# Small TensorE work between expert products in fewer, larger groups, and experts alternating in the last down product

## The chip, the cores and the metric

The kernel runs on one core of one Trainium2 chip. The metric is the device time of one execution in microseconds (us). Three executions of the kernel before took 1856.57, 1856.98 and 1857.13 us, a median of 1856.98 us. A fourth execution was profiled; all rows below come from it.

## The reference

Two layers work on 512 latent tokens and 256 context tokens of width 1024, in float32. Each layer mixes tokens (a bidirectional mLSTM, a convolution and a Fourier mixer between one input and one output projection) and then runs a mixture of 16 experts in which each expert chooses its tokens. The change touches the experts alone:

```python
def expert_choice_ffn(xn, w_router, w_gate, w_up, w_down):
    cap = EC_CAPACITY_FACTOR * n // N_EXPERTS            # 64 of 512 latent, 32 of 256 context tokens
    aff = softmax(xn @ w_router)
    gate, idx = top_k(swapaxes(aff, 1, 2), cap)
    xs = xn[idx]
    hid = silu(xs @ w_gate) * (xs @ w_up)                # each weight 1024 x 1024 per expert
    ys = (hid @ w_down) * gate[..., None]
    return zeros_like(xn).at[idx].add(ys)
...
    h_ctx = h_ctx + cgt2 * expert_choice_ffn(...)        # layer one only
    x = x + gt2 * expert_choice_ffn(...)
return _rms(x, g_final)                                  # after layer two
```

The second layer has no use for its context tokens, so only latent tokens pass its experts. The expert weights are 3 x 16 x 4 MB a layer, 403 MB in the two layers together, of the 513 MB that the kernel reads.

## The kernel before

Experts go in eight pairs p. A pair has three wide products, `gate`, `up` and `down`, each through `wide`, which takes the 1024-deep contraction in four quarters q. A quarter uses two weight tiles of 1 MB, one an expert. The products stand in the order gate 0, up 0, and then for each p: gate p+1, down p, up p+1. In layer one a quarter is 16 float32 matmuls for latent tokens (L1433), a call of `fill(q)`, and 8 matmuls for context tokens (L1443); each occupies 32 of the array's 128 columns, so that four groups of columns hold different products. In layer two it is 8 latent matmuls on 64 columns each (the two experts side by side) and then `fill(q)`. The profile counts each float32 matmul as two instructions.

What `fill` does is the small work, held in lists and taken by `pop`: `turns` fetch the next pair's tokens and transpose them (L1382 in layer one, four transposes and four evictions an item; in layer two `onehot`, L1364, and `turn` as a matmul with a one-hot matrix, L1379); `trans` transposes the hidden activations for the down product (L1485, items of four); `scat` adds results back to the token stream (`sc_`, L1498 on TensorE and L1499 on VectorE). All use the whole array, and each item takes a PSUM bank from `bank67`, banks 6 and 7 in turn. In layer one the first six pairs' results instead go to memory by accumulating indirect DMAs (`down_out`, L1537), and `collect` reads them back (`late`, transposed at L1554 from gate 7 on).

```python
up(0, lambda q: pop(turns))
...
        gate(p + 1, lambda q: (pop(scat), q and pop(trans)))
...
        up(p + 1, lambda q: (q and pop(scat, 2), pop(turns)))
```

The last pair of layer two ends in `down_last`, which makes the down product by quarters qd of 256 output columns. A quarter is 16 matmuls at L1693, in blocks of four: expert 0 for k 0 to 3, expert 1 for k 0 to 3, expert 0 for k 4 to 7, expert 1 for k 4 to 7, with `pop(scat)` behind each block. Quarters 0 and 1 share one PSUM bank, 2 and 3 another. Each quarter is evicted by ScalarE (L1699, the high part) and VectorE (L1700, the rest); `last_sum` then scatters two blocks of 128 columns (L1498, L1499) and squares them (L1675), and `rows` sums the squares on TensorE (L1683) for the final RMS norm, which the last quarter's squares end. After them come L359, L376, the scaling at L1747 and the output.

TensorE's order is the order of the code; the other engines' instructions are ordered by a scheduler. Weights come in one stream on SyncE's queue (L1146, and L1143 for the last pair's down): `load_experts` runs behind each quarter and reloads the buffers as the quarter that used them ends. Layer one has 11 such buffers, so a tile is asked for when the tile eleven places before it has been used; layer two has 16.

Of the kernel before, what the change touches and what calls it, by code (L numbers as in the profile page):

```python
# [15 lines left out]
KB = 8  # L16
# [139 lines left out]
def build(nc, tc, xT, ctxT, params, w_ada, w_gates, w_in, w_out, w_router, w_e_gate, w_e_up, w_e_down,  # L156
# [6 lines left out]
    def body(A, RB, PS, scr, xrow, acc):  # L163
# [233 lines left out]
        for l in range(2):  # L397
# [735 lines left out]
            wtiles, wtaken = [], [0]  # L1133

            def load_experts(firsts=(), most=1000):
                while len(wtiles) < min(wtaken[0] + len(wreg), len(wq), most):
                    w, e, i = wq[len(wtiles)]
                    if last and w is w_e_down and e >= E - 2:
                        t = V(wreg[len(wtiles) % len(wreg)], KB, 256)
                        src = w[l, e, i].rearrange("p (k c) -> p k c", k=KB)  # L1140

                        for k0, k1 in ((0, KB),) if i < 3 else ((0, 4), (4, KB)):
                            sp.dma_start(t[:, k0:k1], src[:, k0:k1])  # L1143
                    else:
                        t = V(wreg[len(wtiles) % len(wreg)], 2, D)
                        r = sp.dma_start(t, w[l, e, i].rearrange("p (a f) -> p a f", a=2))  # L1146
                        after(r, firsts)
                    wtiles.append(t)
# [260 lines left out]

            def bank67():  # L1410
                six[0] += 1
                return B(6 + six[0] % 2)
# [249 lines left out]
            def down_last(p):  # L1662
# [23 lines left out]
                for qd in range(4):  # L1686
# [3 lines left out]
                    for k0 in (0, 4):  # L1690
                        for e in range(2):
                            for k in range(k0, k0 + 4):
                                pe.matmul(b[64 * e:64 * e + 64], hT[:, k, 64 * e:64 * e + 64], w[e][:, k],  # L1693
                                          start=k == 0, stop=k == KB - 1, tile_position=(0, 64 * e))
                            pop(scat)
                    pop(scat, 99)
                    c0 = qd * 256
                    h, lo = (YS[:, j, c0:c0 + 256] for j in range(2))
                    act.activation(h, b, AF.Copy, scale=GP[:, 0, p:p + 1])  # L1699
                    dve.scalar_tensor_tensor(lo, b, GP[:, 0, p:p + 1], h.bitcast(F32), op0=OP.mult, op1=OP.subtract)  # L1700
                    if qd == 2:
                        rows(range(4))
                    scat.extend(last_sum(db) for db in (2 * qd, 2 * qd + 1))
# [16 lines left out]
            up(0, lambda q: pop(turns))  # L1720
            for p in range(NP):
# [4 lines left out]
                if p + 1 < NP:  # L1726
                    fetch_pair(p + 2)
                    gate(p + 1, lambda q: (pop(scat), q and pop(trans)))
# [5 lines left out]
                if p + 1 < NP:  # L1734
                    up(p + 1, lambda q: (q and pop(scat, 2), pop(turns)))
# [109 lines left out]
```

## Time and profile before

| | |
|---|---|
| median of three executions | 1856.98 us |
| profiled execution | 1857.74 us |
| its span, first to last instruction | 1856.0 us |
| around the span | 1.74 us |
| TensorE busy, share of the span | 94% |
| experts of layer one, about | 482 to 1023 us |
| experts of layer two, about | 1368 to 1842 us |

A span counts from the first to the last instruction of the program. A matmul's end is modelled, so a TensorE that counts as busy may be slower than it could be.

### The profile page before, as it was taken

Reading aid. Unit: us, or ns where it says so; the run is one execution under the profiler, and the core shown is the slowest. Engines: PE = TensorE matmul, PEld = TensorE weight load, DVE = VectorE, ACT = ScalarE, POOL = GpSimd, SP = SyncE. Lnnn points to the kernel's source line nnn. Section 1 sums busy time; section 2 is a strip of 40 time slices with the busy share of each in tenths; the row PEclk is TensorE's granted clock in tenths of the full one; section 3 lists DMA queues with packets and bytes.
Section 4 is the critical chain, followed back from the end, with each engine's and each line's share of the span. In section 5 each row is a group of like instructions: output and inputs, shape, how many; then the busy total and the mean of one; then the engine's idle time right before and its main releaser. Section 6 shows DMA issues by size and latency. Waiting matters only on the chain.

```text
span 1856.0 us, 27692 instructions
## 1 busy us (share of the span) xinstructions
PE 1744.3 (94%) x11728; PEld 947.8 (51%) x11728; DVE 627.9 (34%) x1384; ACT 448.5 (24%) x862; POOL 166.0 (9%) x193
## 2 busy tenths in 40 slices
PE   7899999899899999999999989889989999999997
PEld 3678887676333333333233468777644444334433
DVE  4624897323201001001014567956230221121213
ACT  5423354313201101101000553346221001110001
POOL 1122120321101101101100001110000000000000
PEclk8999999899899999999999999999989999999998
DMA  9365344855899999999995112233659999999992
GB/s 346 115 208 193 106 133 137 314 188 209 350 419 402 411 412 403 399 421 391 393 393 217 35 54 79 76 108 129 250 240 421 420 420 421 420 421 420 421 420 99
DMA packets 100668, 529.59 MB, mean 285 GB/s; under 512 B 10176, under 2 KB 21440, under 8 KB 51648
## 3 DMA queue, kind: packets, MB, share of 16 engines
q1 hardware_dynamic: 81920, 459.66, 61.8%
q0 software_dynamic: 18624, 68.17, 11.7%
q8 instruction: 92, 1.51, 0.3%
q14 instruction: 32, 0.26, 0.0%
HBM read 513.10 MB, written 14.68 MB: 284 GB/s over the span
## 4 chain that ended last, share of the span: by engine, by line
PE 70%; DMA 10%; DVE 9%; issue 5%; ACT 2%; SPq 2%; POOL 1%; another core or an unknown queue 0%; DVEq 0%; POOLq 0%; ACTq 0%
PE PS L1433 29%; PE PS L490 16%; PE PS L1443 8%; PE PS L1379 3%; DVE A L1015 2%; PE PS L1498 2%; PE PS L284 1%; PE PS L1693 1%; SPq L309 1%; DMA accc<-A 1%; DMA WP<-w_e_up 1%; DMA A<-w_e_up 1%; DMA A<-w_e_down 1%; DMA A<-w_e_gate 1%; DMA WP<-w_e_gate 1%
## 5 line engine op out<-in xcount | busy, mean ns | idle before, releaser
L490 PE MATMUL PS<-RA,RB 128*128 128x512 f32 (+1 forms) x2352 | 516.4, 367 | 23.6 <-ACT A L973 8.0
L1433 PE MATMUL PS<-A 128*32 128x512 f32 (+1 forms) x2256 | 428.1, 594 | 2.7 <-DMA A<-w_e_up 2.2
L490 PEld LDWEIGHTS PS<-RA,RB 128*128 128x128 f32 x2352 | 379.3, 194 | 99.3 <-issue 20.6
L1433 PE MATMUL PS<-WP,A 128*32 128x512 f32 (+1 forms) x2160 | 373.9, 597 | 0.7 <-DMA WP<-w_e_up 0.7
L1433 PEld LDWEIGHTS PS<-A 128*32 128x32 f32 (+1 forms) x2256 | 128.0, 121 | 224.9 <-issue 213.7
L1433 PEld LDWEIGHTS PS<-WP,A 128*32 128x32 f32 (+1 forms) x2160 | 107.0, 117 | 192.7 <-issue 187.6
L1443 PE MATMUL PS<-WP,A 128*32 128x512 f32 x816 | 112.5, 595 | 0.0
L1015 DVE SCALAR_TENSOR_TENSOR A<-A 128x783 f32<-128x783 f32 (+1 forms) x120 | 107.4, 921 | 0.1
L1499 DVE SCALAR_TENSOR_TENSOR A<-PS,A 128x512 f32<-128x512 f32 x80 | 57.5, 748 | 130.5 <-PE PS L1498 130.5
L1387 ACT ACTIVATE A<-PS,A 128x128 f32<-128x128 f32 x80 | 36.4, 457 | 262.0 <-DVE A L1389 260.8
L1486 ACT ACTIVATE A<-PS 128x512 f32<-128x512 f32 x40 | 23.8, 597 | 306.2 <-PE PS L1485 306.0
L1389 DVE TENSOR_SCALAR A<-PS,A 128x128 f32<-128x128 f32 x80 | 32.6, 409 | 185.8 <-PE PS L1382 93.4
L1443 PE MATMUL PS<-A 128*32 128x512 f32 x656 | 95.3, 607 | 0.0
L422 ACT ACTIVATE RB<-A 128x1024 fp32r<-128x1024 f32 x60 | 63.2, 1057 | 128.4 <-PE PS L490 83.1
L1532 DVE TENSOR_SCALAR A<-PS,A 128x512 f32<-128x512 f32 x6 | 4.5, 750 | 245.6 <-PE PS L1433 245.6
L282 POOL DMA_DIRECT2D A<-w_ada x80 | 60.1, 754 | 211.2 <-PE PS L284 134.2
L1506 DVE SCALAR_TENSOR_TENSOR RB<-PS,A,RB 128x512 fp32r<-128x512 f32 x18 | 13.5, 750 | 163.7 <-ACT RB L1505 162.8
L1379 PE MATMUL PS<-A 128*128 128x128 f32 x512 | 64.0, 285 | 5.0 <-DVE A L1499 4.5
L425 DVE TENSOR_TENSOR RB<-A,RB 128x1024 fp32r<-128x1024 f32 x50 | 60.8, 1221 | 21.0 <-ACT RB L422 20.6
L1379 PEld LDWEIGHTS PS<-A 128*128 128x128 f32 x512 | 61.0, 199 | 12.9 <-DVE A L1499 9.8
L1443 PEld LDWEIGHTS PS<-WP,A 128*32 128x32 f32 x816 | 26.8, 109 | 50.8 <-issue 50.8
L1498 PE MATMUL PS<-RB 128*128 128x512 f32 x160 | 51.7, 431 | 1.0 <-DVE A L1499 0.4
(334 smaller groups left out, 1583.8 us busy)
## 6 DMA issues: line engine op xcount, KB each, us to landing
A<-w_e_gate SPq DMA_DIRECT2D x75, 1024.0 KB, 14.3
A<-w_e_up SPq DMA_DIRECT2D x66, 1024.0 KB, 13.0
WP<-w_e_down SPq DMA_DIRECT2D x63, 1024.0 KB, 14.3
A<-w_e_down SPq DMA_DIRECT2D x63, 1024.0 KB, 16.0
WP<-w_e_up SPq DMA_DIRECT2D x62, 1024.0 KB, 13.0
WP<-w_e_gate SPq DMA_DIRECT2D x53, 1024.0 KB, 14.9
A<-w_ada POOLq DMA_DIRECT2D x80, 512.0 KB, 5.5
A<-w_in SPq DMA_DIRECT2D x44, 512.0 KB, 3.7
```

The costliest lines, as they stand in the source:

```text
L282: after(eng.dma_start(w, src[r, hf, k]), firsts if hf == 0 and k < len(ring.regs) else ())
L422: whi.append(act.activation(h, raw[i], AF.Copy))
L425: wlo.append(eng.tensor_tensor(lo, raw[i], h.bitcast(F32), OP.subtract))
L490: pe.matmul(banks[s][:, :LEN[s]], w[:, k], xin[:, j, k, OFF[s]:OFF[s] + LEN[s]], start=k == k0 and i == 0, stop=k == k1 and i == 2)
L1015: dve.scalar_tensor_tensor(o, i, wcol, o, op0=OP.mult, op1=OP.add)
L1379: pe.matmul(b[:, j], XT[2 + c][:, db * 128:db * 128 + 128], onehots[i][:, c], start=c == 0, stop=c == 3)
L1387: act.activation(dst[:, db], b[:, j], AF.Identity, bias=sh_, scale=sc_)
L1389: dve.tensor_scalar(dst[:, db], b[:, j], sc_, sh_, op0=OP.mult, op1=OP.add)
L1433: pe.matmul(B(o + hf)[c:c + wd, :], lhs(k, e)[:, c % 64:c % 64 + wd], w[e][:, a, hf * 512:hf * 512 + 512], start=k == 0, stop=k == KB - 1, ...
L1443: pe.matmul(B(o + 2)[32 * g:32 * g + 32, :], lhsc(k, e), w[e][:, a, hf * 512:hf * 512 + 512], start=k == 0, stop=k == KB - 1, tile_positio ...
L1498: pe.matmul(b, YS[:, j, db * 128:db * 128 + 128], PM if pm is None else pm, start=j == 0, stop=j == 1)
L1499: dve.scalar_tensor_tensor(X[LAT][:, db], b, MOD[l][:, LAT, 40 + db:41 + db], X[LAT][:, db], op0=OP.mult, op1=OP.add)
```

## The change

It has four parts. First, the lists are popped at other quarters and more at a time. In layer one `turns` come two together behind quarters 0 and 2 of up, and of the three `trans` two come together behind quarter 1 of gate and one behind quarter 2. In layer two gate pops two `trans` at quarter 1, and up pops four `scat` and the one-hot item at quarter 1, and two `turns` and four `scat` at quarter 3. Second, `bank67` has four banks to go round in layer two. Third, `down_last` alternates the experts at every k, pops nothing inside a product, makes the first `rows` behind quarter 3 instead of 2, and pops each quarter's sums behind the next quarter's product. Fourth, the halves of the last two weight tiles are asked for in turn.

```diff
--- before.py
+++ after.py
@@ -1130,7 +1130,7 @@
             for q in range(NP):
                 order += [(w_e_gate, q + 1)] * (q + 1 < NP) + [(w_e_down, q)] + [(w_e_up, q + 1)] * (q + 1 < NP)
             wq = [(w, 2 * q + e, i) for w, q in order for i in range(4) for e in range(2)]
-            wtiles, wtaken = [], [0]
+            wtiles, wtaken, halves = [], [0], []
 
             def load_experts(firsts=(), most=1000):
                 while len(wtiles) < min(wtaken[0] + len(wreg), len(wq), most):
@@ -1139,8 +1139,14 @@
                         t = V(wreg[len(wtiles) % len(wreg)], KB, 256)
                         src = w[l, e, i].rearrange("p (k c) -> p k c", k=KB)
 
-                        for k0, k1 in ((0, KB),) if i < 3 else ((0, 4), (4, KB)):
-                            sp.dma_start(t[:, k0:k1], src[:, k0:k1])
+
+                        halves.append((t, src))
+                        if i < 3:
+                            sp.dma_start(*halves.pop())
+                        elif len(halves) == 2:
+                            for k0 in (0, 4):
+                                for t_, s_ in halves:
+                                    sp.dma_start(t_[:, k0:k0 + 4], s_[:, k0:k0 + 4])
                     else:
                         t = V(wreg[len(wtiles) % len(wreg)], 2, D)
                         r = sp.dma_start(t, w[l, e, i].rearrange("p (a f) -> p a f", a=2))
@@ -1407,9 +1413,12 @@
 
             six = [0]
 
+
+            small = (6, 2, 7, 5) if last else (6, 7)
+
             def bank67():
                 six[0] += 1
-                return B(6 + six[0] % 2)
+                return B(small[six[0] % len(small)])
 
             sets = [0]
 
@@ -1687,19 +1696,21 @@
                     w = wtiles[wtaken[0]:wtaken[0] + 2]
                     wtaken[0] += 2
                     b = B(o + qd // 2)[:, qd % 2 * 256:qd % 2 * 256 + 256]
-                    for k0 in (0, 4):
+
+                    for k in range(KB):
                         for e in range(2):
-                            for k in range(k0, k0 + 4):
-                                pe.matmul(b[64 * e:64 * e + 64], hT[:, k, 64 * e:64 * e + 64], w[e][:, k],
-                                          start=k == 0, stop=k == KB - 1, tile_position=(0, 64 * e))
-                            pop(scat)
-                    pop(scat, 99)
+                            pe.matmul(b[64 * e:64 * e + 64], hT[:, k, 64 * e:64 * e + 64], w[e][:, k],
+                                      start=k == 0, stop=k == KB - 1, tile_position=(0, 64 * e))
                     c0 = qd * 256
                     h, lo = (YS[:, j, c0:c0 + 256] for j in range(2))
+
+                    if qd == 0:
+                        pop(scat, 99)
                     act.activation(h, b, AF.Copy, scale=GP[:, 0, p:p + 1])
                     dve.scalar_tensor_tensor(lo, b, GP[:, 0, p:p + 1], h.bitcast(F32), op0=OP.mult, op1=OP.subtract)
-                    if qd == 2:
+                    if qd == 3:
                         rows(range(4))
+                    pop(scat, 99)
                     scat.extend(last_sum(db) for db in (2 * qd, 2 * qd + 1))
                 rows((4, 5))
                 pop(scat, 99)
@@ -1717,7 +1728,7 @@
 
             gate(0, lambda q: pop(turns, 99))
             fetch_pair(1)
-            up(0, lambda q: pop(turns))
+            up(0, lambda q: pop(turns, (1, 0, 0, 2)[q] if last else 2 * (1 - q % 2)))
             for p in range(NP):
                 pop(turns, 99)
                 if p >= NACC:
@@ -1725,14 +1736,19 @@
                     late.clear()
                 if p + 1 < NP:
                     fetch_pair(p + 2)
-                    gate(p + 1, lambda q: (pop(scat), q and pop(trans)))
+                    gate(p + 1, (lambda q: q == 1 and pop(trans, 2)) if last else
+                         (lambda q: (pop(scat), pop(trans, (0, 2, 1, 0)[q]))))
                 pop(trans, 99)
                 if p == NP - 1:
                     down_last(p) if last else down_mid(p)
                 else:
                     down(p, lambda q: pop(scat))
                 if p + 1 < NP:
-                    up(p + 1, lambda q: (q and pop(scat, 2), pop(turns)))
+
+                    if last:
+                        up(p + 1, lambda q: (q == 3 and pop(turns, 2), q % 2 and pop(scat, 4), q == 1 and pop(turns)))
+                    else:
+                        up(p + 1, lambda q: (q and pop(scat, 2), q % 2 or pop(turns, 2)))
             wp_close()
             mem.free([[r for r in wreg if r[2] is mem], sl_r, ht_r, ys_r, pm_r, xs_r])
             if not last:
```

The first place is TensorE in the experts of layer one, gate 1. The numbers of lines are those of each kernel: L1485 of before is L1494 of the changed one (`trans`), L1433 is L1442 and L1443 is L1452. Before:

```order
L1433 MATMUL PS<-A 32x512 x16
L1485 MATMUL PS<-A 128x128 x4
L1443 MATMUL PS<-A 32x512 x8
L1433 MATMUL PS<-A 32x512 x16
L1485 MATMUL PS<-A 128x128 x4
L1443 MATMUL PS<-A 32x512 x8
```

The changed kernel at the same place:

```order
L1442 MATMUL PS<-A 32x512 x16
L1494 MATMUL PS<-A 128x128 x8
L1452 MATMUL PS<-A 32x512 x8
L1442 MATMUL PS<-A 32x512 x16
L1494 MATMUL PS<-A 128x128 x4
L1452 MATMUL PS<-A 32x512 x8
```

The item of four that stood in the third quarter now stands with the first, and the last of the three moves up one quarter, so that gate 1 has two interruptions where it had three. In all of layer one's experts up to down 5, single items of `trans` and `turns` become pairs at fifteen places, and at one more in up 6.

The second place is TensorE at the end of layer two, from the last quarters of up 7 into `down_last`. L1498 (`scat`) is L1507 in the changed kernel, L1693 is L1702; A and WP are buffers of the two experts' weights. Before:

```order
L1498 MATMUL PS<-RB 128x512 x4
L1433 MATMUL PS<-A 64x512 x8
L1498 MATMUL PS<-RB 128x512 x4
L1485 MATMUL PS<-A 128x128 x8
L1693 MATMUL PS<-A 64x256 x4
L1498 MATMUL PS<-RB 128x512 x2
L1693 MATMUL PS<-WP_8537,A 64x256 x4
L1498 MATMUL PS<-RB 128x512 x2
L1693 MATMUL PS<-A 64x256 x4
L1693 MATMUL PS<-WP_8537,A 64x256 x4
```

The changed kernel:

```order
L1507 MATMUL PS<-RB 128x512 x8
L1442 MATMUL PS<-A 64x512 x16
L1507 MATMUL PS<-RB 128x512 x8
L1494 MATMUL PS<-A 128x128 x8
L1702 MATMUL PS<-A 64x256
L1702 MATMUL PS<-WP_8537,A 64x256
```

All eight scatters of pair 6 now stand in up 7, four behind its last quarter, and in `down_last` the two experts' matmuls follow each other one by one, with none of the small work between them.

The third place is the end of `down_last`, on TensorE: L1683 (`rows`) is L1692 in the changed kernel. Before:

```order
L1683 MATMUL PS<-A 32x512 x4
L1693 MATMUL PS<-WP_8542,A 64x256 x4
L1498 MATMUL PS<-RB 128x512 x2
L1693 MATMUL PS<-A 64x256 x4
L1498 MATMUL PS<-RB 128x512 x2
L1693 MATMUL PS<-WP_8542,A 64x256 x4
L1693 MATMUL PS<-A 64x256 x4
L1683 MATMUL PS<-A 32x512 x2
L1498 MATMUL PS<-RB 128x512 x4
L1683 MATMUL PS<-A 32x512 x2
```

The changed kernel, from the last matmul of the last quarter on:

```order
L1702 MATMUL PS<-A 64x256
L1692 MATMUL PS<-A 32x512 x4
L1507 MATMUL PS<-RB 128x512 x4
L1692 MATMUL PS<-A 32x512 x2
L1507 MATMUL PS<-RB 128x512 x4
L1692 MATMUL PS<-A 32x512 x2
```

The first four sums of squares and the scatters of quarter 2 stood ahead of or inside the last quarter's product, and stand behind it now.

On VectorE the changed kernel's add for the first scatter of quarter 1 stands ahead of the second eviction of quarter 2 (L1508 is L1499 of before, L1710 is L1700):

```order
L1710 SCALAR_TENSOR_TENSOR RB<-PS,A,RB 128x256
L1508 SCALAR_TENSOR_TENSOR A<-PS,A 128x512
L1710 SCALAR_TENSOR_TENSOR RB<-PS,A,RB 128x256
L1508 SCALAR_TENSOR_TENSOR A<-PS,A 128x512 x2
L1710 SCALAR_TENSOR_TENSOR RB<-PS,A,RB 128x256
L1508 SCALAR_TENSOR_TENSOR A<-PS,A 128x512
L1710 SCALAR_TENSOR_TENSOR RB<-PS,A,RB 128x256
```

The four L1710 are the evictions of quarters 0 to 3. Before, both adds of a quarter stood ahead of the next eviction.

## Rows read from the trace of the kernel before

**Rows 1.** Stretches: length, busy of PE, PEld, DVE, ACT, POOL; clock, DMA share, GB/s.

```profile
486.00:900.00 414.00, 414.00 (x3764) 128.34 (x3760) 30.79 (x60) 48.45 (x87) 35.33 (x27) 1.00 1.01 408
920.00:940.00 20.00, 15.69 (x123) 4.62 (x116) 2.82 (x4) 0.00 (x0) 1.10 (x2) 0.83 1.02 414
1357.00:1366.00 9.00, 6.37 (x27) 5.73 (x28) 4.16 (x17) 0.51 (x2) 0.00 (x0) 0.50 0.00 0
1380.00:1800.00 420.00, 412.64 (x2055) 178.59 (x2053) 78.72 (x142) 41.53 (x73) 0.00 (x0) 1.00 1.01 420
```

**Rows 2.** Where SyncE's queue issued one tile, 775.0 to 775.4: issue and landing.

```profile
L1146 SPq DMA_DIRECT2D WP<-w_e_gate x1: 328/328/328, 775.1 to 775.1; - x1
...
DMA to landing us min/median/max: 14.9/14.9/14.9
```

**Rows 3.** Timeline of TensorE in layer one: start, us, instructions; first use of that tile.

```profile
796.25 2.33 PE L1433 MATMUL PS<-WP,A 128*32 128x512 f32 x20
```

**Rows 4.** Chain of work through layer two: start us, us, what.

```profile
1668.12 19.83 DMA WP<-w_e_gate
...
1767.65 19.85 DMA A<-w_e_up
```

**Rows 5.** Timeline of TensorE in layer one, quarters with and without small work.

```profile
610.29 3.62 PE L1433 MATMUL PS<-WP,A 128*32 128x512 f32 x32
...
616.17 3.62 PE L1433 MATMUL PS<-WP,A 128*32 128x512 f32 x32
...
621.32 1.04 PE L1433 MATMUL PS<-A 128*32 128x512 f32 x8
```

**Rows 6.** The same in gate 7, a quarter with two items together.

```profile
948.78 3.62 PE L1433 MATMUL PS<-WP,A 128*32 128x512 f32 x32
952.33 0.66 PE L1554 MATMUL PS<-A 128*128 128x128 f32 x4
952.82 0.60 PE L1485 MATMUL PS<-A 128*128 128x128 f32 x4
...
955.09 0.61 PE L1433 MATMUL PS<-WP,A 128*32 128x512 f32 x4
```

**Rows 7.** Waits of TensorE, 920 to 940: us in total, times, longest.

```profile
PE PS L1554 <- DMA A<-accl: 4.3, 1, 4.3
```

**Rows 8.** Timeline of TensorE from the end of up 7 into `down_last`.

```profile
1801.05 1.19 PE L1498 MATMUL PS<-RB 128*128 128x512 f32 x4
1802.63 1.31 PE L1485 MATMUL PS<-A 128*128 128x128 f32 x8 [0.38 <-DVE A L1499]
1804.02 1.94 PE L1693 MATMUL PS<-A 128*64 128x256 f32 x8
...
1810.44 0.38 PE L1693 MATMUL PS<-A 128*64 128x256 f32 x1
1810.49 0.38 PE L1693 MATMUL PS<-WP,A 128*64 128x256 f32 x1
...
1813.10 1.94 PE L1693 MATMUL PS<-WP,A 128*64 128x256 f32 x8 [1.15 <-DVE RB L1700]
```

**Rows 9.** Timeline of all engines behind the last product.

```profile
1836.88 1.05 PE L1683 MATMUL PS<-A 128*32 128x512 f32 x4
...
1837.49 0.48 DVE L1700 SCALAR_TENSOR_TENSOR RB<-PS,A,RB 128x256 fp32r<-128x256 f32 x1 [2.55 <-ACT RB L1699]
...
1838.63 1.41 DVE L1499 SCALAR_TENSOR_TENSOR A<-PS,A 128x512 f32<-128x512 f32 x2 [0.65 <-PE PS L1498]
1839.47 1.29 ACT L1675 ACTIVATE A<-A 128x512 f32<-128x512 f32 x2 [2.01 <-DVE A L1499]
...
1840.15 1.28 PE L1683 MATMUL PS<-A 128*32 128x512 f32 x3 [1.10 <-ACT A L1675]
```

**Rows 10.** Timeline of TensorE at the start of layer two's experts.

```profile
1361.13 6.46 PE L1379 MATMUL PS<-A 128*128 128x128 f32 x32 [0.44 <-DVE A L1366]
...
1371.69 3.84 PE L1379 MATMUL PS<-A 128*128 128x128 f32 x32
```

## The prediction

> **What bounds the kernel now.** I read first the busy time by stretch, then, stage by stage, what the queue of the weights, TensorE and the tail wait for.
>
> In the experts of layer one both sides look full. TensorE is busy 414.00 of 414 us at a granted clock of 1.00, and the DMA engines are busy all the time at 408 GB/s [rows 1]. Which of them leads is seen in one tile's way: it is asked for at 775.1, lands 14.9 later, at 790.0, and is first used at 796.25 [rows 2, 3]. It lies ready for 6.2 us, and TensorE waited for no weight in that stretch. So TensorE sets the pace there, and the weights follow with some 6 us to spare. The request goes out when a buffer comes free; most of the 14.9 us are a queue ahead of it, so the transfers never starve either.
>
> In layer two it is the other way round. From 1380 to 1800 the DMA engines move 420 GB/s without a gap [rows 1], and the chain of waits runs through the queue: six times from 1668.12 to 1767.65 a tile takes 19.85 us from issue to landing and its landing lets out the next [rows 4]. The tile at the end of each step belongs to the next product in the stream, eight tiles on. So 48 tiles take the 119.4 us from the first issue to the last landing, 2.49 us each. The last landing of that chain, 1787.50, is the fourth of up 7's eight tiles; the eighth then lands at about 1797.5, and the last of the last down eight tiles later, at 1817.4. Before 1668 TensorE lags behind the weights, but the transfers are saturated already, so nothing that TensorE does sooner in that layer brings the last byte sooner. What is left is the stretch behind the last weights of up 7, where TensorE, ScalarE and VectorE follow each other.
>
> **Grouping in layer one.** A quarter without small work takes 621.32 - 616.17 = 5.15 us, one with one item of four transposes 616.17 - 610.29 = 5.88 [rows 5], one with two items side by side 955.09 - 948.78 = 6.31 [rows 6]. The first item costs 0.73, the second 0.43. An item that joins another instead of standing alone saves 0.30. The order shows fifteen such up to down 5 and one in up 6. The sixteenth is worth nothing: TensorE then waits 4.3 us for the sums that come back from memory [rows 7], and these hang on down 5's end, so it would only wait longer. 15 x 0.29 (0.30 by these rows, rounded times) is **4.3 us**, if the weights keep up. Up to 796 eleven of the fifteen have been saved, 3.2 us, and the tile of [rows 2, 3] still has 3.0 to spare. Everything behind layer one's experts, layer two's first request for weights included, moves 4.3 us ahead.
>
> **Grouping in layer two, four banks.** The seven interruptions of a pair become three, some 4 x 0.29 = 1.2 us a pair, and fewer waits for a bank. I cost this at nothing, because the weights hide it [rows 1, 4]; without that cover the seven pairs would give about 8 us.
>
> **The last pair**, in the time of before. The last quarter of up 7 still waits for its weights, so it still ends at 1801.05 [rows 8]. Behind it stand four scatters for two: four matmuls take 1.19, eight add at most another 1.19. Since the transposes waited 0.38 for VectorE before, I take 0.5, and `down_last` starts at 1804.5 instead of 1804.02.
>
> Its products gain most. Alone, a block of eight instructions takes 1.94, of which 0.38 is the last one's own length: 0.22 an instruction [rows 8]. Where two experts' blocks touch, the one's instruction starts at 1810.44 and the other's at 1810.49, both of 0.38 [rows 8]: the two halves of the array work side by side. In the changed order all 32 instructions of a quarter pair up like that: 15 x 0.216 + 0.05 + 0.38 = 3.67 us. The Trainium skill (TensorEngine Tiling (Array Packing), Theoretical Speedup) gives up to 2x for 64 columns. The rows agree where two streams touch; by the rule alone the 32 instructions of 0.216 would take 3.46 us a quarter and the sum would be 0.8 us lower, because it leaves out the length of the last instruction.
>
> Quarter 0 ends at 1808.2. Quarter 1 has the same bank and waits for the eviction, 1.15 as before [rows 8]: 1809.3 to 1813.0. Two scatters (1.19) then fill, and quarter 2, in another bank, runs from 1814.1 to 1817.7. Behind it two scatters start at 1817.65; VectorE adds the first before it may evict quarter 2: 0.70 to the add's start (1838.63, less 1837.93 where the sums of 1836.88 end and the scatters begin), 0.7 for the add (half of 1.41), 0.48 for the eviction [rows 9]. Quarter 3 starts at 1819.6, behind its weights, and ends at 1823.3. Before, it ended at about 1836.95, as the first `rows` of [rows 9] began. **13.6 us sooner.**
>
> Something is given back. Before, the last squares followed the product by 3.2 us (the second of two at 1840.13, [rows 9]). Now four sums (1.05), two scatters with add and square, two sums that wait for these squares, and only then the last two scatters stand behind the product: add at 1.75, squares 0.84 behind their adds at 2.6 and 3.25, sums 0.68 behind each (1840.15 less 1839.47) and 1.05 long, scatters from 5.0 on, add at 5.7, squares at 6.5 and 7.2 [rows 9]. That is **4.0 us more**: the last sums wait on TensorE for ScalarE, and the last scatters stand queued behind them. The tail nets 9.6. The order of the halves is worth nothing while quarter 3 starts behind the last landing.
>
> **Sum.** 4.3 + 9.6 = 13.9 from 1857.74, which is 1843.8 for a profiled execution. That execution stands 0.76 above the median, so I forecast **1843.1**.
>
> **Rivals.**
> - *The weights swallow layer one's gain.* The DMA engines were full there as well [rows 1]. Then only the tail pays: 1847.4. Against it stand the 6.2 us to spare.
> - *The clock falls (the slower case).* TensorE runs at its upper level, 2.4 GHz, throughout layer two, but fell after the wait of 4.3 us (0.83 in 920 to 940, [rows 1, 7]). If the longer waits for weights and evictions drop it to 1.2 GHz (0.50 in 1357 to 1366), work costs 6.46 for 3.84 [rows 1, 10], at least 1.7 times. Some 25 us of work in the last 40 would cost 17 more, and up 7 would fall behind its weights by about 3: 1863. It decides from about 20 us of work at the lower level on. Against it: in the last waits for weights of the kernel before the clock stayed at 1.00 [rows 1]. The Trainium skill (TensorE: Matmul & The Clock Gate, HAM oscillation — how this bites in real kernels) describes just this, a matmul loop that waits for transfers and starts cold each time; the trace agrees for the one wait of 4.3 us and for none of the short ones.
> - *Alternation does not pair.* If each instruction took 0.216 alone, a quarter would be 7.1, the product would end where it did, and the 4.0 would eat layer one's 4.3: 1856.7, no change. The 1810.44 and 1810.49 speak against it.
> - *Layer two pays too*, if requests for buffers and not bandwidth held the weights: 8 more, 1835.1. The 420 GB/s without a gap speak against it.
>
> **How the numbers follow.** The forecast has 0.77, the weights' rival 0.10, the clock 0.04, no pairing 0.03, layer two 0.03, and 0.03 is left for what I do not see. The low end: quarter 3's second half cannot start before the last landing, 1817.4, and takes 1.9, so the products could end 4.0 us sooner than I have it: 1839.1. The high end is the weights' rival with the wait for one more eviction (1.15): 1848.5. A measurement tells some 0.2%, 3.7 us, from no change. Faster by more has the forecast, the weights, layer two and a part of the rest, 0.91; within it no pairing and a part of the clock, 0.05; slower 0.04.
>
> **What would show it.** Right: quarters of layer one with two items at 6.3 us and fifteen interruptions fewer by down 5, whose end is 4 us sooner; DMA share 1.0 and 420 GB/s in layer two's experts; L1702 at 3.7 us a quarter; evictions as the wait between quarters 0 and 1 and between 2 and 3; L1692 waiting for ScalarE behind the last product. Wrong: TensorE waiting for weights in layer one, a granted clock below 1.00 between 1380 and 1830, or L1702 at 7 us.

## The result, and the profile after

The changed kernel takes 1842.81 us, the median of five executions from 1839.43 to 1846.18. Five of the kernel before, run beside them, have a median of 1857.13. The ratio is 0.9909, with a 95% interval of 0.9883 to 0.9935: faster, by 12 to 22 us by that interval, and by 14.3 between the medians. The forecast was 1843.1. The profiled execution took 1842.09, with a span of 1840.3.

Layer one's experts and layer two's, by stretches (the view of [rows 1]):

```profile
486.00:900.00 414.00, 414.00 (x3804) 131.45 (x3800) 31.72 (x60) 48.19 (x88) 37.59 (x29) 1.00 1.02 410
918.00:938.00 20.00, 15.57 (x130) 5.34 (x125) 2.64 (x4) 1.20 (x2) 0.94 (x2) 0.91 1.02 412
1375.00:1795.00 420.00, 405.67 (x2054) 181.05 (x2051) 76.80 (x142) 40.90 (x73) 0.00 (x0) 1.00 1.01 420
1795.00:1828.00 33.00, 27.96 (x184) 15.12 (x181) 11.47 (x18) 9.96 (x17) 0.00 (x0) 1.00 0.48 194
```

In layer one TensorE is still busy all the time, and does 40 instructions more in the same 414 us. In layer two the DMA engines still move 420 GB/s, and TensorE is busy 405.67 of 420 us instead of 412.64: what it saves it waits. The granted clock is 1.00 there and in the tail.

The waits of TensorE in layer two, 1375 to 1796 (us in total, times, longest), show for whom:

```profile
PE PS L1442 <- DMA A<-w_e_up: 5.9, 5, 1.3
...
PE PS L1442 <- DMA WP<-w_e_up: 4.0, 3, 1.3
```

The kernel before, from 1375 to 1801:

```profile
PE PS L1433 <- DMA A<-w_e_up: 2.2, 2, 1.3
PE PS L1433 <- DMA WP<-w_e_up: 0.7, 1, 0.7
```

So the stretch had 2.9 us of waits for weights before and has 9.9 now. TensorE's timeline around the end of down 5 in layer one answers to [rows 5, 7] (L1388, a `turn`, was L1382, and L1563, `late`, was L1554):

```profile
897.46 3.62 PE L1442 MATMUL PS<-A 128*32 128x512 f32 x32
901.01 1.09 PE L1388 MATMUL PS<-A 128*128 128x128 f32 x8
...
903.77 3.62 PE L1442 MATMUL PS<-WP,A 128*32 128x512 f32 x32
...
908.92 3.62 PE L1442 MATMUL PS<-WP,A 128*32 128x512 f32 x32
...
926.86 1.09 PE L1563 MATMUL PS<-A 128*128 128x128 f32 x4 [4.02 <-DMA A<-accl]
```

Two items side by side make a quarter of 6.31 (903.77 - 897.46), none one of 5.15 (908.92 - 903.77). The wait for accl, the sums in memory that `collect` reads back, is 4.0 instead of 4.3.

TensorE's timeline through the tail answers to [rows 8, 9] (L1702 was L1693, L1507 was L1498, L1692 was L1683, the squares at L1684 were L1675, VectorE's eviction at L1710 was L1700):

```profile
1796.09 2.11 PE L1507 MATMUL PS<-RB 128*128 128x512 f32 x8
...
1799.37 0.43 PE L1702 MATMUL PS<-A 128*64 128x256 f32 x1 [0.30 <-ACT A L1495]
1799.38 0.43 PE L1702 MATMUL PS<-WP,A 128*64 128x256 f32 x1
...
1804.20 3.67 PE L1702 MATMUL PS<-WP,A 128*64 128x256 f32 x32 [1.15 <-DVE RB L1710]
1807.80 1.19 PE L1507 MATMUL PS<-RB 128*128 128x512 f32 x4
1808.92 3.67 PE L1702 MATMUL PS<-WP,A 128*64 128x256 f32 x32
1812.53 1.20 PE L1507 MATMUL PS<-RB 128*128 128x512 f32 x4
1814.50 0.43 PE L1702 MATMUL PS<-WP,A 128*64 128x256 f32 x1 [0.77 <-DVE RB L1710]
...
1818.10 1.06 PE L1692 MATMUL PS<-A 128*32 128x512 f32 x8
1819.10 1.21 PE L1507 MATMUL PS<-RB 128*128 128x512 f32 x4
1821.41 1.64 PE L1692 MATMUL PS<-A 128*32 128x512 f32 x4 [1.10 <-ACT A L1684]
1822.98 1.20 PE L1507 MATMUL PS<-RB 128*128 128x512 f32 x4
1825.22 1.71 PE L1692 MATMUL PS<-A 128*32 128x512 f32 x4 [1.04 <-ACT A L1684]
1827.61 1.05 PE L359 MATMUL PS<-A 128*128 128x1 f32 x8 [0.69 <-ACT A L356]
```

The two experts' instructions start 0.01 apart, a quarter takes 3.67, quarters 1 and 3 wait 1.15 and 0.77 for the eviction ahead of them, and behind the last product (1818.10) the row sums wait for ScalarE's squares, 1.10 and 1.04.

**Where the 15.7 us of the span went**, by start times in the two traces:

| stretch | before | after | difference |
|---|---|---|---|
| start to the first expert product | 481.77 | 482.42 | +0.65 |
| to the last latent matmul of layer one's up 7 | 520.95 | 515.39 | -5.56 |
| to layer two's first expert product | 365.38 | 364.77 | -0.61 |
| to `down_last`'s first product | 435.92 | 436.79 | +0.87 |
| to its last product | 32.55 | 18.42 | -14.13 |
| to L359 | 5.98 | 9.82 | +3.84 |
| to the end | 13.41 | 12.67 | -0.74 |

These stretches tell more than medians here. One kernel's executions lie up to 14 us apart, and in the profiles below much of it arises ahead of the experts, in code that no kernel changes: the first expert product starts between 481.66 and 491.06. The stretches with the change in them repeat far better. From layer one's second quarter to the quarter that waits for accl, all five profiles with the old order give 434.34 us (923.38 - 489.04 before), and eight of nine with the new one 429.76 (919.22 - 489.46 after). The ninth, of sums_and_banks, gives 430.89: two early quarters are 0.3 and 0.8 longer there, behind a first quarter that took 5.18 us where the other profiles have 5.67 to 7.27. Its view of waits shows no wait for weights in them, and the cause stays open.

### The profile page after: what moved, and what is told of

Read it like the earlier page. It is cut to its first block, busy times and chain, and to the rows that moved or that the text cites. A ratio compares the mean times of both kernels' runs of the same rounds, so it can differ in the third digit from the quotient of the medians.

```text
span 1840.3 us, 27705 instructions
## 1 busy us (share of the span) xinstructions
PE 1716.8 (93%) x11728; PEld 942.8 (51%) x11728; DVE 625.7 (34%) x1384; ACT 446.6 (24%) x862; POOL 165.4 (9%) x193
## 4 chain that ended last, share of the span: by engine, by line
PE 61%; DMA 19%; DVE 9%; issue 5%; ACT 2%; SPq 2%; POOL 1%; another core or an unknown queue 0%; DVEq 0%; POOLq 0%; ACTq 0%
PE PS L1442 23%; PE PS L490 16%; PE PS L1452 8%; DMA WP<-w_e_down 3%; DMA A<-w_e_up 3%; DVE A L1015 2%; DMA A<-w_e_gate 2%; DMA WP<-w_e_gate 2%; DMA A<-w_e_down 2%; DMA WP<-w_e_up 2%; PE PS L284 1%; PE PS L1385 1%; SPq L309 1%; DMA accc<-A 1%; PE PS L1507 1%
## 5 line engine op out<-in xcount | busy, mean ns | idle before, releaser
L1442 PE MATMUL PS<-A 128*32 128x512 f32 (+1 forms) x2256 | 425.7, 593 | 6.5 <-DMA A<-w_e_up 5.9
L1442 PE MATMUL PS<-WP,A 128*32 128x512 f32 (+1 forms) x2160 | 370.5, 597 | 4.0 <-DMA WP<-w_e_up 4.0
L1442 PEld LDWEIGHTS PS<-A 128*32 128x32 f32 (+1 forms) x2256 | 127.3, 121 | 241.2 <-issue 222.3
L1442 PEld LDWEIGHTS PS<-WP,A 128*32 128x32 f32 (+1 forms) x2160 | 108.7, 117 | 197.1 <-issue 185.4
L1452 PE MATMUL PS<-WP,A 128*32 128x512 f32 x816 | 112.3, 594 | 0.0
L1452 PE MATMUL PS<-A 128*32 128x512 f32 x656 | 94.3, 601 | 0.0
L1508 DVE SCALAR_TENSOR_TENSOR A<-PS,A 128x512 f32<-128x512 f32 x80 | 56.5, 745 | 87.5 <-PE PS L1507 86.7
L1486 DVE TENSOR_TENSOR A<-PS,A 128x512 f32<-128x512 f32 x32 | 22.1, 692 | 110.3 <-PE PS L1442 110.3
L1452 PEld LDWEIGHTS PS<-WP,A 128*32 128x32 f32 x816 | 27.9, 110 | 54.6 <-issue 54.6
```

Source lines behind the costliest of these rows:

```text
L1442: pe.matmul(B(o + hf)[c:c + wd, :], lhs(k, e)[:, c % 64:c % 64 + wd], w[e][:, a, hf * 512:hf * 512 + 512], start=k == 0, stop=k == KB - 1, ...
L1452: pe.matmul(B(o + 2)[32 * g:32 * g + 32, :], lhsc(k, e), w[e][:, a, hf * 512:hf * 512 + 512], start=k == 0, stop=k == KB - 1, tile_positio ...
L1508: dve.scalar_tensor_tensor(X[LAT][:, db], b, MOD[l][:, LAT, 40 + db:41 + db], X[LAT][:, db], op0=OP.mult, op1=OP.add)
```

## The experiments

The times of a kernel and of the kernel before beside it come from one chip. In the table, "layer two" runs from its first expert product to `down_last`'s first, "products" from there to the start of `down_last`'s last instruction, "behind" from there to L359; all are differences of start times in one profile each. Line numbers shift with the edits: L1703, L1704 and L1705 below are L1702 of the changed kernel, L1711 and L1712 are L1710, and layer2_only has the numbers of the kernel before.

| kernel | median | ratio to before (95%) | layer two | products | behind |
|---|---|---|---|---|---|
| before | | | 435.92 | 32.55 | 5.98 |
| changed | 1842.81 | 0.9909 (0.9883-0.9935) | 436.79 | 18.42 | 9.82 |
| tail_only | 1851.36 | 0.9960 (0.9940-0.9980) | 435.82 | 19.90 | 9.80 |
| layer1_only | 1852.75 | 0.9959 (0.9944-0.9975) | 435.89 | 32.55 | 5.98 |
| layer2_only | 1857.00 | 0.9991 (0.9975-1.0008) | 436.32 | 29.32 | 5.98 |
| blocks_back | 1852.58 | 0.9958 (0.9942-0.9974) | 437.00 | 22.53 | 9.80 |
| rows_at_2 | 1844.38 | 0.9929 (0.9905-0.9952) | 437.37 | 20.78 | 9.32 |
| banks_alternate | 1837.44 | 0.9903 (0.9877-0.9929) | 436.96 | 17.41 | 9.80 |
| sums_inside | 1838.80 | 0.9904 (0.9880-0.9929) | 436.95 | 19.73 | 6.01 |
| sums_and_banks | 1837.95 | 0.9899 (0.9871-0.9926) | 437.13 | 17.49 | 5.99 |
| best | 1839.12 | 0.9897 (0.9880-0.9913) | 437.41 | 19.34 | 5.92 |
| block_lengths | one run, 1850.34 | | 437.30 | 21.61 | 9.81 |
| half_weights | 1853.63 | 0.9975 (0.9963-0.9987) | 429.27 | 32.54 | 5.99 |
| half_weights_grouped | 1836.94 | 0.9882 (0.9861-0.9903) | 418.21 | 29.32 | 5.97 |

The kernel before ran at 1860.01 beside the first four of these kernels (tail_only to blocks_back), at 1857.27 beside the next four and at 1857.78 beside the last four.

**The parts one by one.** The changed kernel with the old pops and two banks:

```diff
-            small = (6, 2, 7, 5) if last else (6, 7)
+            small = (6, 7)
-            up(0, lambda q: pop(turns, (1, 0, 0, 2)[q] if last else 2 * (1 - q % 2)))
+            up(0, lambda q: pop(turns))
...
+                    gate(p + 1, lambda q: (pop(scat), q and pop(trans)))
...
+                    up(p + 1, lambda q: (q and pop(scat, 2), pop(turns)))
```

> The kernel before with the change's down_last and the order of the last tiles' halves, the small work in the experts' products grouped as before and on two banks. Mine: the tail stands alone and is worth what it showed in the changed kernel's trace, 10.7 us (the end moved by 15.7, up 7's last quarter by 5.0), so about 1846.5, with the L1702 products at 3.6 to 3.7 us a quarter (the term on record is 9.6, so 1847.5). Rival: the tail's gain leans on the earlier or better grouped layer two (four banks, eight scatters together ahead of it); then less than 8 us, 1849 or more.

Products and what is behind them come to 29.70 us for 38.53 before: 8.8 gained, less than either of my numbers. The two scatters that up 7 leaves over now stand between quarters 0 and 1, in front of the eviction, and quarter 1 waits 1.50 for it:

```profile
1813.03 1.19 PE L1507 MATMUL PS<-RB 128*128 128x512 f32 x4
1815.72 3.67 PE L1702 MATMUL PS<-WP,A 128*64 128x256 f32 x32 [1.50 <-DVE RB L1710]
```

So 1.46 of the changed kernel's tail is lent by layer two's pops (28.24 there). By the trace the rival's "less than 8" did not come, but its reason holds for this part; the ratio, 4 to 11 us, can't tell the two apart.

The kernel before with layer one's new pops:

```diff
-            up(0, lambda q: pop(turns))
+            up(0, lambda q: pop(turns, 1 if last else 2 * (1 - q % 2)))
...
-                    gate(p + 1, lambda q: (pop(scat), q and pop(trans)))
+                    gate(p + 1, lambda q: (pop(scat), q and pop(trans)) if last else
+                         (pop(scat), pop(trans, (0, 2, 1, 0)[q])))
...
-                    up(p + 1, lambda q: (q and pop(scat, 2), pop(turns)))
+                    up(p + 1, lambda q: (q and pop(scat, 2), pop(turns)) if last else
+                       (q and pop(scat, 2), q % 2 or pop(turns, 2)))
```

> The kernel before with only layer one's pops changed. Mine: 4.3 us by the term on record, 4.9 by the shift of up 7's end in the changed kernel's trace, so 1852 to 1853, and up 7's last scatters 4 to 5 us sooner. Rival (the weights swallow it): 1857, no change. Second rival: the 4.9 are in part fewer windows at the lower clock behind the stall for accl, which this kernel need not have; then about 1853 to 1854, with down 5's end 3.9 sooner and nothing behind it.

The interval is 4.6 to 10.4 us faster, which excludes the weights' rival. From the second quarter to the one that waits for accl it takes 429.76, as the changed kernel: 4.58 saved. Behind the wait, in gate 7, something is lost. The changed kernel's timeline there:

```profile
930.63 3.61 PE L1442 MATMUL PS<-A 128*32 128x512 f32 x32
934.16 0.66 PE L1563 MATMUL PS<-A 128*128 128x128 f32 x4
934.66 0.60 PE L1494 MATMUL PS<-A 128*128 128x128 f32 x4
935.67 0.66 PE L1494 MATMUL PS<-A 128*128 128x128 f32 x4 [0.41 <-DVE A L1565]
...
937.99 0.60 PE L1442 MATMUL PS<-A 128*32 128x512 f32 x2
```

The second `trans` waits 0.41 for VectorE, and the quarter takes 7.36 (937.99 - 930.63) where two items took 6.31 [rows 6]; two quarters on, where one item is gone, 0.44 come back. That is a loss of 0.6. With the wait for accl and the granted clock behind it (0.83 to 0.99 between 918 and 938), which differ from run to run, the way from the second quarter to the last latent matmul of up 7 is 513.1 us in the mean of the five profiles with the old order (512.55 to 513.68) and 509.2 in the mean of the nine with the new one (507.79 to 510.31): 3.9 sooner. Of the shift of 4.9 that my second number came from, some 1 us is thus a difference between executions, as the second rival has it (1853 to 1854).

The kernel before with layer two's new pops and the four banks:

```diff
-                return B(6 + six[0] % 2)
+                return B((6, 2, 7, 5)[six[0] % 4] if last else 6 + six[0] % 2)
...
+                    gate(p + 1, (lambda q: q == 1 and pop(trans, 2)) if last else
+                         (lambda q: (pop(scat), q and pop(trans))))
...
+                    if last:
+                        up(p + 1, lambda q: (q == 3 and pop(turns, 2), q % 2 and pop(scat, 4), q == 1 and pop(turns)))
```

> The kernel before with only layer two's pops and its four banks changed. Mine: nothing, 1857 within 2, because the weights' stream at 420 GB/s sets the pace; TensorE only waits longer for weights. Rival (requests for buffers, not bandwidth, hold the weights): 8 us sooner, 1849.

The stretch of layer two is 0.4 longer, not 8 shorter, so the 8 fall. But the tail behind it is 3.2 shorter, and the expectation of nothing was wrong there, though the times (0.9975 to 1.0008) can't tell that from nothing. Its timeline shows why:

```profile
1799.25 1.29 PE L1693 MATMUL PS<-A 128*64 128x256 f32 x5 [0.30 <-ACT A L1486]
...
1802.71 1.24 PE L1693 MATMUL PS<-WP,A 128*64 128x256 f32 x5
1805.10 1.94 PE L1693 MATMUL PS<-WP,A 128*64 128x256 f32 x8 [1.15 <-DVE RB L1700]
1806.97 0.73 PE L1498 MATMUL PS<-RB 128*128 128x512 f32 x2
1807.63 1.94 PE L1693 MATMUL PS<-WP,A 128*64 128x256 f32 x8
```

Quarter 1 still has a scatter behind each of its first two blocks of eight: 2.53 us a block (1807.63 - 1805.10), of which the scatter takes 0.66. Quarter 0 has none, since up 7 left no scatter over, and its 32 instructions take 4.70 us (1799.25 to 1803.95), though they stand in the old blocks.

**What pairs the experts.** The changed kernel with the old blocks:

```diff
-                    for k in range(KB):
+                    for k0 in (0, 4):
                         for e in range(2):
+                            for k in range(k0, k0 + 4):
```

> The changed kernel with the blocks of four instructions an expert back in down_last, all pops and the halves as changed. Mine (the experts side by side make the gain): a quarter takes 6.7 to 7.2 instead of 3.67, 3.1 to 3.5 more, and less than four times that on the end because some waits shrink: 1852 to 1856. Rival (that nothing interrupts a product any more makes the gain): within 2 of the changed kernel, 1843 to 1845.

```profile
1806.46 1.29 PE L1703 MATMUL PS<-A 128*64 128x256 f32 x5 [0.30 <-ACT A L1495]
1807.38 0.43 PE L1703 MATMUL PS<-WP,A 128*64 128x256 f32 x1
...
1812.30 4.70 PE L1703 MATMUL PS<-WP,A 128*64 128x256 f32 x32 [1.14 <-DVE RB L1711]
```

Both were wrong. The median, 1852.58, falls into my range, but the kernel before was some 3 us slower beside it, and in its profile the first expert product already starts 8.6 later than in the changed kernel's; the stretches decide. A quarter takes 4.70, 1.03 more than 3.67 and far from 7; the products end 4.1 later than the changed kernel's (22.53 for 18.42), not 9 to 13. The rows show that the second expert's block starts at 1807.38 with the fifth of the first expert's eight instructions, and the rest runs beside it. The kernel before did the same only where no scatter stood between two blocks. So of the 14.1 us that the products gained, 4.1 are the alternation where nothing interrupts it (alternation around scatters left inside was not tried), and 10.0 are that nothing stands inside a product; of these 3.2 come with layer two's pops alone. Part of the 10.0 is work that only moved: two scatters into up 7, two scatters and the first row sums behind the last product, where they count in the 3.8 that is longer. At 0.66 a scatter and 1.0 for the row sums (1819.10 - 1818.10 in the changed kernel) that is some 3.6, an estimate; the rest, over 6 us, is that the experts' blocks run side by side, with the shorter scatters and waits that come with it.

Blocks of other lengths in the four quarters of one kernel:

```diff
-                    for k in range(KB):
+                    n = (2, 3, 8, 1)[qd]
+                    for k0 in range(0, KB, n):
                         for e in range(2):
+                            for k in range(k0, min(k0 + n, KB)):
```

> The changed kernel with blocks of 2, 3, 8 and 1 matmuls an expert in quarters 0, 1, 2 and 3 of down_last (a matmul counts as two instructions). Blocks of 4 took 4.63 a quarter in blocks_back, 1 takes 3.60. Mine: an instruction starts with the fourth one ahead of it in the program at the earliest, so a block of 2 pairs wholly (3.6), a block of 3 starts 0.43 late once (4.0), a block of 8 2.65 late (6.2). Rival (half of a block passes before the other expert's can start, which blocks of 4 show as well): 4.0, 4.2 and 5.4.

```profile
1808.90 4.16 PE L1704 MATMUL PS<-WP,A 128*64 128x256 f32 x32 [1.15 <-DVE RB L1712]
...
1814.13 6.31 PE L1704 MATMUL PS<-WP,A 128*64 128x256 f32 x32
1820.37 1.21 PE L1507 MATMUL PS<-RB 128*128 128x512 f32 x4
```

These lengths hold 0.07 of the last instruction that the next one overlaps. Blocks of 3 take 4.16 and of 8 6.31, that is 4.09 and 6.24 to the next instruction: the expected 4.0 and 6.2, against 4.2 and 5.4 of the rival, which falls with the blocks of 8. Blocks of 2 took 3.72 by the first start and the last end (1804.03 to 1807.75), 0.05 over the alternating order.

**What is given back, and what would keep it.** The changed kernel with the first row sums a quarter sooner:

```diff
-                    if qd == 3:
-                        rows(range(4))
                     pop(scat, 99)
+                    if qd == 2:
+                        rows(range(4))
```

> The changed kernel with the first four sums of squares (rows(range(4))) behind quarter 2's pops instead of behind quarter 3's product. Mine: the eight row matmuls (1.00 us in the changed kernel's trace) leave the path behind the last product, but stand in front of quarter 3 and wait there for the squares of quarter 1's sums; these come at 1815.8 where quarter 3 now starts at 1814.5, so quarter 3 starts about 1.5 later and the gain is eaten: between 1.0 slower and 1.0 faster than the changed kernel, 1842 to 1844. Rival (the 4.0 on record as given back come from this move): 3 or more faster, 1840 or less.

```profile
1816.05 1.21 PE L1507 MATMUL PS<-RB 128*128 128x512 f32 x4
1817.19 3.21 PE L1692 MATMUL PS<-A 128*32 128x512 f32 x8
```

Slower by 1.9 (30.10 for 28.24): the row sums stand 3.1 us in front of quarter 3, because they wait for squares, and take only 0.5 away behind it. That is more than I allowed, and it excludes the rival: the move of `rows` is not what gives back the 4 us.

Alternate banks:

```diff
-                    b = B(o + qd // 2)[:, qd % 2 * 256:qd % 2 * 256 + 256]
+                    b = B(o + qd % 2)[:, qd // 2 * 256:qd // 2 * 256 + 256]
```

> The changed kernel with the quarters of down_last on alternate banks (0 and 2 on one, 1 and 3 on the other), so that no quarter waits for the eviction of the one ahead of it. Mine: the waits of 1.15 (quarter 1) and 0.77 (quarter 3) go, but quarter 3 can't start before the last weights (first halves about 1810.5, last 1812.48), so 1.9 in the sum and 1.5 to 2 at the end: about 1841. Rival (the last landing sets quarter 3's end anyway, or the sums ahead of it wait instead): 0, 1843.

```profile
1807.19 3.67 PE L1702 MATMUL PS<-WP,A 128*64 128x256 f32 x30 [0.28 <-DMA WP<-w_e_down]
...
1811.91 3.97 PE L1702 MATMUL PS<-WP,A 128*64 128x256 f32 x32
```

1.0 of the 1.9 came. Quarter 1 now waits 0.28 for its weights, and quarter 2 takes 3.97: behind the eviction stands the landing, as the rival said, though not for all of it.

Quarter 2's sums inside quarter 3's product (in this kernel and the next the squares of blocks 4 and 5 take the buffers of 0 and 1 before those are summed, so the norm is of other data, by the same instructions):

```diff
+                        if qd == 3 and k == 4:
+                            pop(scat, 99)
                         for e in range(2):
...
-                rows((4, 5))
                 pop(scat, 99)
-                rows((6, 7))
+                rows(range(4, 8))
```

> The changed kernel with quarter 2's two sums popped in the middle of quarter 3's product (after the first half of its contraction) and the last four row sums together at the end. Mine: what is given back behind the last product (sums, squares, row sums of quarter 2 in series with those of quarter 3, 1819.1 to 1822.98) goes under it; the product gets 1.5 longer, the stretch from its end to the row sums' end loses about 4: 2.5 faster than the changed kernel, 1840. Rival: the interruption waits for quarter 2's eviction and VectorE, and eats it: within 1 of the changed kernel.

```profile
1822.68 1.06 PE L1692 MATMUL PS<-A 128*32 128x512 f32 x8
1823.67 1.20 PE L1507 MATMUL PS<-RB 128*128 128x512 f32 x4
1824.81 2.88 PE L1692 MATMUL PS<-A 128*32 128x512 f32 x8
1828.38 1.05 PE L359 MATMUL PS<-A 128*128 128x1 f32 x8 [0.69 <-ACT A L356]
```

One round of scatters, squares and sums is left behind the product instead of two: 6.01 for 9.82. The product is 1.3 longer, so 2.5 are gained (25.74 for 28.24), as expected. This shows what the 3.8 given back are: quarter 2's round in series with quarter 3's.

> Both of the last two: alternate banks and quarter 2's sums inside quarter 3's product. Mine: they add, since one takes waits ahead of quarter 3 and the other work behind it: 4 to 4.5 faster than the changed kernel, about 1838.5. Rival: with the waits gone the sums of quarter 2 come too late for the middle of quarter 3 and TensorE waits there: not over 2.5 together, 1840.

23.48 for 28.24, 4.8 sooner: they add, and with quarter 1's weights in time each got its whole share (1.9 and 2.5) or a little more. As a kernel that computes the reference, it needs the first row sums ahead of the squares that take their buffers (shown against the changed kernel, beside the edits above):

```diff
+                        if qd == 3 and k == 4:
+                            rows((0, 1))
+                            pop(scat, 99)
...
                     if qd == 3:
-                        rows(range(4))
+                        rows((2, 3))
```

> The changed kernel with quarters of down_last on alternate banks, quarter 2's sums in the middle of quarter 3's product, the row sums of the blocks whose squares' buffers these need ahead of them, and the last four row sums together. Mine: from the first product of down_last to L359 23.5 to 24.5 us, where the changed kernel takes 28.2: some 4 faster, about 1838.5. Rival: the row sums inside the product wait for squares of quarter 1 and eat half of it: 26.

```profile
1812.42 0.65 PE L1705 MATMUL PS<-WP,A 128*64 128x256 f32 x2
1813.28 3.67 PE L1705 MATMUL PS<-WP,A 128*64 128x256 f32 x30 [0.22 <-DMA WP<-w_e_down]
...
1819.88 1.05 PE L1692 MATMUL PS<-A 128*32 128x512 f32 x4
1820.86 1.21 PE L1507 MATMUL PS<-RB 128*128 128x512 f32 x4
...
1823.88 1.05 PE L1692 MATMUL PS<-A 128*32 128x512 f32 x4
```

25.26 for 28.24: 3.0 sooner than the changed kernel, not 4 to 4.7. Its row sums waited for no square (the rival's reason), but four instructions on two column groups take 1.05 where eight on four groups took 1.06, so cutting them in two costs 1.0; and quarter 2 lost 0.86 to its weights. Its ratio, 0.9897, beats the kernel before by some 19 us (16 to 22); against the changed kernel's 0.9909 the intervals overlap, and only the trace tells the two apart.

**What layer two's grouping, with its four banks, is worth without its cover.** The kernel before with half of layer two's weight bytes, and the same with layer two's pops and banks as in layer2_only:

```diff
-                        r = sp.dma_start(t, w[l, e, i].rearrange("p (a f) -> p a f", a=2))
+                        src = w[l, e, i].rearrange("p (a f) -> p a f", a=2)
+                        r = sp.dma_start(t[:, :1], src[:, :1]) if last and len(wtiles) >= 24 else sp.dma_start(t, src)
```

> The kernel before, but from the 25th weight tile of layer two on (the last down apart) only the first half of each tile is fetched and the other half is what lay there: the same instructions on half the bytes. Mine: TensorE then sets layer two's pace, and the stretch from its first expert product to down_last's first, 435.9 us before, gets some 10 to 30 shorter, with no wait for weights.

> The same, half the bytes of layer two's weights, with layer two's pops and four banks as changed. Mine (the weights hide the grouping's worth): against half_weights the stretch from the first expert product to down_last's first is 7 to 9 us shorter, where with whole weights it was 0.4 longer; and down_last's products end some 3 sooner behind it, as in layer2_only. Rival (grouping saves nothing there, or the larger groups wait for evictions and VectorE): within 2 of half_weights in that stretch.

From 1500 to 1600 in both, first the old order, then the grouped:

```profile
1500.00:1600.00 100.00, 98.49 (x504) 43.97 (x504) 22.00 (x40) 9.83 (x18) 0.00 (x0) 1.00 0.61 210
```

```profile
1500.00:1600.00 100.00, 98.55 (x518) 45.90 (x516) 21.31 (x40) 9.59 (x18) 0.00 (x0) 1.00 0.65 222
```

With the DMA engines at some 0.6 no wait for weights is left, and layer two's stretch is 6.7 us shorter than with whole weights, below the 10 to 30: TensorE's own work was closer behind the weights than I thought. Now the grouping is worth 11.1 us there (418.21 for 429.27), and 3.2 more in the products. The rival's "nothing" falls; my 7 to 9 were too little.

## Why the prediction was right

**Term 1, layer one, 4.3: measured 3.9 in the mean of the profiles.** Up to down 5's end, for which the term was worked out, it came in full: 408.00 us from the second quarter on instead of 412.30. An item that joins another saves 0.286 (4.58 over sixteen), against the 0.29 I took. What I left out is gate 7, which now loses 0.6 because two `trans` meet the sums there. Whether the wait for accl swallows the sixteenth can't be told: it differs by more than that between profiles. The weights kept up in the changed kernel's profile, with no wait for them between 486 and 900, and layer1_only shows that the part pays alone.

**Term 2, layer two, 0.** Its stretch became 0.9 longer with the change. I had 0.5, for the four scatters behind up 7 instead of two; from there to `down_last` it is 0.3 (1799.37 - 1796.09 = 3.28 for 1804.02 - 1801.05 = 2.97). The rest lies ahead, where the stretches of the nine kernels with the new pops and whole weights differ by 1.1 (436.32 to 437.41), and was not traced further. The reason is shown from both sides: TensorE's waits for weights grow from 2.9 to 9.9, and with half the bytes the same edit gives 11.1. The 8 us named for the case without cover were too few. What the four banks add to the new pops was not tried apart. What I did not see is that these pops also clear quarter 0 of the tail: 3.2 us alone, 1.5 beside the new `down_last`.

**Term 3, products 13.6 sooner: measured 13.3, 14.1 less the 0.9 by which `down_last` starts later.** The waits came where they were put, 1.15 and 0.77. But the step that explains it, "In the changed order all 32 instructions of a quarter pair up like that", credits the order with what mostly came from the removed interruptions. Blocks pair too once nothing stands between them: 4.70 a quarter, not 7. So the rival without pairing was priced wrongly: by the stretches the products would have been 4.1 later, a time near 1847, not 1856.7. The Trainium skill (TensorEngine Tiling (Array Packing), Theoretical Speedup) gives up to 2x for 64 columns; the starts 0.01 apart agree, and blocks_back and block_lengths show that the order of issue decides how much of it comes.

**Term 4, 4.0 given back: measured 3.8**, by the mechanism named: sums waiting for squares, with the last scatters queued behind them. rows_at_2 and sums_inside tell it from the mere move of `rows`.

**The sum.** 13.9 was forecast for the profiled execution, 15.7 came. 3.9 + 13.3 - 3.8 = 13.4 is the change's. The other 2.3 are differences between two executions in what the change does not touch: 1.7 in layer one's first quarter and around the wait for accl (5.56 less 3.9), 0.6 between the layers and 0.7 behind L359, less the 0.65 lost ahead of the experts. So that the forecast lies within 0.3 us of the median is partly luck: the changed kernel's five executions lie 6.75 apart. The clock's rival did not come: 1.00 up to 1828.

Not tried is the order of the two halves by itself. In the changed kernel the last landing is at 1812.48 and quarter 3 starts at 1814.50, so it had nothing to give there.

## What to carry to other kernels

Keep small full-array work between the products of column-tiled streams, not inside them, and alternate the streams at every one or two matmuls: first look for what stands between the blocks, then at their order. The exception is work that a chain behind the last product waits for: in sums_inside one interruption made the product 1.3 longer and took 3.8 off what follows it. Grouping such work pays where TensorE leads (0.29 an item here) and nothing where the weights do, which a pair of runs on half the bytes shows. Where executions differ by more than the edit is worth, compare the lengths of the stretches that hold it.

## What the runs showed of the hardware

TensorE starts the next stream's instruction while earlier ones of another column group still wait their turn, but only so far ahead. All five block lengths agree with one rule, that an instruction begins with the fourth one ahead of it in the program at the earliest: blocks of 1, 2, 3, 4 and 8 matmuls took 3.67, 3.72, 4.16, 4.70 and 6.31 us a quarter. That is read from starts in this program, at one shape (64 columns, 256 wide, float32); why it is four was not tried.
